# A gather, running sum and projection on one core: sums and carry by pairs of tiles in place of tile by tile, and gathers whose run-ahead grows from three pairs to eight

## The chip, the cores and the metric

The kernel runs on one core of a Trainium2 chip. The metric is the device time of one execution in microseconds (us). Several runs are taken; the median counts. The profile is that of one execution.

## The reference

For each of 16 batches, 2048 sorted row numbers pick rows of 512 floats out of 4096; the running sum over the picked rows is multiplied by a matrix of 512 x 512.

```python
B, S, N, D = (16, 4096, 2048, 512)
gathered = x[b_idx, indices, :].copy()      # (16, 2048, 512)
cs = np.cumsum(gathered, axis=1)
return np.matmul(cs, w).astype(np.float32)
```

The kernel reads 67 MB of picked rows and writes 67 MB of output.

## The kernel before

The 32,768 picked rows are cut into T = 256 tiles of P = 128 rows. Two tiles make a pair (R = 2), so there are G = 128 pairs; a batch has 16 tiles, or 8 pairs. Each engine has a list of instructions written out by hand, and a small class `Lane` puts a wait before an instruction when a semaphore must have reached a value that this engine has not yet waited for.

**POOL** (`gather`, L102 to L117) issues one indirect DMA a tile: 128 rows of x, cast to fp16 on the way, into one half of one of eight pair buffers `g16`. Tile t may be gathered when the buffer of its pair g is free, that is when `s_a` (L104) has reached 2(g+1) - 16: the sums of pair g - 8 are done. The first four tiles take their row numbers from a small early load; the others from `idxg`, which is made at the start by PE transposes (L256).

**PE** makes two kinds of matmuls. `sums(t)` (L119 to L134) multiplies the gathered tile with a mask `ut` of ones and zeros, 128 columns for each of the four 128-wide chunks of D. The result is the running sum inside the tile, transposed, in one of four PSUM buffers `pa` (NA = 4, one bank each). The columns are dealt so that even and odd output rows of the pair stand apart. The last of the four matmuls increments `s_a`. `project(g, j)` (L153 to L164) multiplies one half of the summed pair with the fp16 matrix `w16`, four matmuls of 512 columns into `pb` (NB = 2 buffers of two banks). The last one of a pair increments `s_b`.

**DVE** (`carry`, L136 to L151) adds to each tile's sums the last column of the tile before and writes fp16 into `cst`, one instruction of 128 x 512 a tile; at the first tile of a batch it only copies. It increments `s_d`. Each carry needs the one before it.

**ACT** (`drain`, L166 to L168) copies a pair's projection from `pb` to one of eight output buffers `ob` and increments `s_e`. **SP** (`store`, L170 to L174) writes it out, 512 KB a DMA.

PE's order is fixed: sums run AH = 2 pairs ahead of projections, and in the loop (L281 to L284) a tile's sums alternate with one half of a projection: `sums(2(g+2))`, `project(g,0)`, `sums(2(g+2)+1)`, `project(g,1)`. PE waits at three places: a tile's sums wait for the gather (`s_g`) and for the carry of four tiles before (L123); inside the first tile of a pair, after its first matmul, for the drain that frees the projection's buffer (`s_e`, L126); and `project(g, j)` waits for `s_d` to reach 2(g+1) + j (L154), so that the first half waits for its own pair's carries and the second half for one carry more. Where the loop ends (L285 to L295) the order is written out: first half of the last pair but two and so on, with the last two tiles' sums between them.

Of the kernel before, what the change touches and what calls it, by code (L numbers as in the profile page):

```python
# [7 lines left out]
P = 128  # L8
FP32 = mybir.dt.float32
FP16 = mybir.dt.float16  # L10
# [17 lines left out]
def kernel(  # L28
# [7 lines left out]
    nc = tc.nc  # L36

    B, S, D = x.shape
    N = indices.shape[1]
    R = 2  # L40
    Q = P // R
    DC = D // P
    NT = N // P
    T = B * NT
    G = T // R
    GB = NT // R
    KI = T // P
    FIRST = 2 * R
    NG = 16
    NA = 4  # L50
    NB = 2
    NC = 4
    NO = 8
    AH = 2
    assert D == 512 and N % (R * P) == 0 and T % P == 0

    x_flat = x.rearrange("b s d -> (b s) d")

    const = ctx.enter_context(tc.tile_pool(name="const", bufs=1))
    ps = ctx.enter_context(tc.tile_pool(name="ps", bufs=1, space=bass.MemoryType.PSUM))  # L60
# [4 lines left out]
    idxg = const.tile([P, KI, P], U32)  # L65
    w32 = const.tile([P, DC, D], FP32)
    w16 = const.tile([P, DC, D], FP16)
    ut = const.tile([P, R, Q], FP16)
    ident = const.tile([P, P], FP32)
    zeros = const.tile([P, D], FP16)  # L70
    spare = const.tile([P, 1], FP16)
    g16 = [const.tile([P, R, D], FP16, name=f"g16_{i}") for i in range(NG // R)]
    cst = [const.tile([P, DC, R, P], FP16, name=f"cst{i}") for i in range(NC)]
    ob = [const.tile([P, R, D], FP32, name=f"ob{i}") for i in range(NO)]
    pa = [ps.tile([P, DC, R, Q], FP32, name=f"pa{i}") for i in range(NA)]
    pb = [ps.tile([P, R, D], FP32, name=f"pb{i}") for i in range(NB)]

    ctx.enter_context(tc.tile_critical(no_gpsimd_drain=True))  # L78
# [1 line left out]
    def sem(name):  # L80
        return tc.alloc_semaphore(name)
# [11 lines left out]
    s_a = sem("s_a")  # L93
    s_d = sem("s_d")
# [3 lines left out]
    pool, pe, dve, act, sp = (  # L98
        Lane(e) for e in (nc.gpsimd, nc.tensor, nc.vector, nc.scalar, nc.sync)
    )  # L100

    def gather(t):  # L102
        g, r = divmod(t, R)
        pool.need(s_a, R * (g + 1) - NG)  # L104
        if t < FIRST:
            pool.need(s_first[g], 16)
            ap = idx_first[:, t, 0:1]
        else:
            pool.need(s_prep, t // P + 1)
            ap = idxg[:, t // P, t % P : t % P + 1]  # L110
        nc.gpsimd.indirect_dma_start(  # L111
            out=g16[g % (NG // R)][:, r, :],
            out_offset=None,
            in_=x_flat,
            in_offset=bass.IndirectOffsetOnAxis(ap=ap, axis=0),
            element_offset=(t // NT) * S * D,
        ).then_inc(s_g[t % NG], 16)  # L117

    def sums(t):  # L119

        g, r = divmod(t, R)
        pe.need(s_g[t % NG], 16 * (t // NG + 1))
        pe.need(s_d, t - NA + 1)  # L123
        for c in range(DC):
            if r == 0 and c == 1:
                pe.need(s_e, g - AH - NB + 1)  # L126
            mm = nc.tensor.matmul(  # L127
                out=pa[t % NA][:, c],
                lhsT=g16[g % (NG // R)][:, r, c * P : (c + 1) * P],
                rhs=ut[:],  # L130
                start=(c == 0),
                stop=(c == DC - 1),
            )
        mm.then_inc(s_a, 1)  # L134

    def carry(t):  # L136
        g, r = divmod(t, R)
        dve.need(s_a, t + 1)
        dst = cst[g % NC][:, :, :, r * Q : (r + 1) * Q]
        if t % NT == 0:  # L140
            nc.vector.tensor_copy(out=dst, in_=pa[t % NA][:]).then_inc(s_d, 1)  # L141
            return
        e = (r - 1) % R
        last = cst[(t - 1) // R % NC][:, :, R - 1, e * Q + Q - 1 : e * Q + Q]
        dve.need(s_d, t)
        nc.vector.tensor_tensor(  # L146
            out=dst,
            in0=pa[t % NA][:],
            in1=last.unsqueeze(2).broadcast_to([P, DC, R, Q]),
            op=mybir.AluOpType.add,  # L150
        ).then_inc(s_d, 1)  # L151

    def project(g, j):  # L153
        pe.need(s_d, min(R * (g + 1) + j, T))  # L154
        for c in range(DC):
            mm = nc.tensor.matmul(  # L156
                out=pb[g % NB][:, j],
                lhsT=cst[g % NC][:, c, j, :],
                rhs=w16[:, c, :],
                start=(c == 0),  # L160
                stop=(c == DC - 1),
            )
        if j == R - 1 or g == G - 1:
            mm.then_inc(s_b, 1)  # L164
# [11 lines left out]
    def drain_last(j, lane, copy):  # L176
        g = G - 1
        lane.need(s_o[g % NO], 16 * (g // NO))
        lane.need(s_b, g + j + 1)
        copy(out=ob[g % NO][:, j], in_=pb[g % NB][:, j]).then_inc(s_el[j], 1)  # L180
# [9 lines left out]
    with nc.allow_non_contiguous_dma(reason="a few indices, one per partition"):  # L190
        for k, eng in enumerate((nc.sync, nc.scalar)):
            t = k * R
            eng.dma_start(
                out=idx_first[:, t : t + R, :],
                in_=indices[0, t * P : (t + R) * P]
# [4 lines left out]
    for k in range(KI):  # L200
        nc.sync.dma_start(
            out=idx64[:, k, :], in_=idx_rows[k * P : (k + 1) * P, :]
# [8 lines left out]
    for j in range(R):  # L211
# [7 lines left out]
        out=ident[:],  # L219
        in_=ident[:],  # L220
# [3 lines left out]
        pattern=[[-1, P]],  # L224
# [3 lines left out]
        out=ut[:],  # L228
        in_=ut[:],
        compare_op=mybir.AluOpType.is_ge,  # L230
        fill=0.0,
        base=0,
        pattern=[[1, R], [R, Q]],
        channel_multiplier=-1,
    ).then_inc(s_ut, 1)
    for t in range(T):
        gather(t)
# [15 lines left out]
    for k in range(KI):  # L253
# [3 lines left out]
            out=pb[k % NB][:, 0, :P], in_=idxf[:, k, :], identity=ident[:]  # L257
# [5 lines left out]
    for c in range(DC // 2, DC):  # L263
        dve.need(s_w[c], 16)
        nc.vector.tensor_copy(out=w16[:, c, :], in_=w32[:, c, :]).then_inc(s_wc, 1)  # L265
    for t in range(T):
        carry(t)
    drain_last(0, dve, nc.vector.tensor_copy)


# [1 line left out]
    for t in range(R):  # L272
        sums(t)
    pe.need(s_prep, KI)
    pe.need(s_wc, DC)
    for j in range(R):
        project(0, j)
        sums(R + j)
    for t in range(2 * R, R * (AH + 1)):
        sums(t)  # L280
    for g in range(1, G - AH - 1):  # L281
        for j in range(R):
            sums(R * (g + AH) + j)
            project(g, j)  # L284
    pe.need(s_e, G - NB - 2)  # L285
    project(G - 3, 0)
    project(G - 3, 1)
    sums(T - 2)
# [48 lines left out]
```

## Time and profile before

| what | value |
|---|---|
| median of 3 runs | 401.83 us (401.7 to 401.89) |
| the profiled execution's own time | 401.7 us |
| its span, first to last instruction | 400.0 us |
| PE busy | 322.6 us (81%) |
| POOL busy | 241.5 us (60%) |
| DVE busy | 178.9 us (45%) |
| ACT busy | 128.4 us (32%) |
| DMA queue of the gathers | 36864 packets, 33.57 MB, 59.2% of 16 engines |
| DMA queue of the stores and loads | 19712 packets, 68.43 MB, 44.1% of 16 engines |
| mean granted PE clock | 0.917 |

The profile divides the span into 40 slices of 10 us; each digit is a share in tenths. "Idle before, releaser" in a row tells how long the engine stood still before the instruction and what ended it; "remote" and "unknown queue" mean that the profile found no instruction of this core that ended just then, and "issue" that it waited for nothing the profile shows. Matmuls overlap, so a matmul's duration is longer than its place in the stream. The shares of the two DMA queues add up to more than 100%, because packets of one engine overlap in part.

### The profile page before, as it was taken

What the parts mean: (1) busy time and instruction counts of PE and PEld (TensorE: products, weight loads), DVE (VectorE), ACT (ScalarE), POOL (GpSimd) and SP (SyncE); (2) the same over time, 40 slices, a digit from 0 to 9 for tenths busy, and PEclk for the clock granted to TensorE, in tenths of its full rate; (3) what the DMA queues carried; (4) which work ended last, traced back from release to release, by engine and by line L of the source; (5) the groups of instructions that cost most, each with busy time, mean ns of one, the idle gap of its engine ahead of it and who ended that gap; (6) DMA issues with size and microseconds to landing.
All of it is one profiled execution on the core that took longest, in us unless ns stands there. A gap on an engine that the chain in (4) does not pass through costs nothing.

```text
span 400.0 us, 5354 instructions
## 1 busy us (share of the span) xinstructions
PE 322.6 (81%) x2064; PEld 167.6 (42%) x2064; DVE 178.9 (45%) x264; ACT 128.4 (32%) x132; POOL 241.5 (60%) x264
## 2 busy tenths in 40 slices
PE   6456976797989787978789886879897898798995
PEld 2222533344544344534445443445354444354552
DVE  2214444554444454535444445554444444554552
ACT  2102423432332233233233224323332333432342
POOL 6774665666666566666666656666665765666400
PEclk9955999988989989899989899999899898988999
DMA  7986999999999999999999999999999999999985
GB/s 180 152 113 108 278 263 260 287 253 270 279 276 262 257 257 284 263 279 259 273 280 278 255 265 275 262 259 278 290 258 255 263 284 259 276 265 268 282 306 225
DMA packets 56874, 102.34 MB, mean 256 GB/s; under 512 B 6801, under 2 KB 39825, under 8 KB 56849
## 3 DMA queue, kind: packets, MB, share of 16 engines
q0 software_dynamic: 36864, 33.57, 59.2%
q1 hardware_dynamic: 19712, 68.43, 44.1%
q8 instruction: 16, 0.26, 0.3%
q14 instruction: 10, 0.07, 0.0%
q10 hardware_dynamic: 272, 0.00, 0.0%
HBM read 68.42 MB, written 67.11 MB: 339 GB/s over the span
## 4 chain that ended last, share of the span: by engine, by line
PE 74%; issue 10%; another core or an unknown queue 7%; ACT 4%; DMA 2%; DVE 1%; ACTq 0%; DVEq 0%; SPq 0%
PE pb L156 57%; PE pa L127 17%; ACT ob L168 4%; DVE cst L146 1%; DMA g<-in_x_dram,idx_first 1%; DMA idx_first<-in_indices_dram 0%; ACT ob L180 0%; ACTq L23 0%; DVEq L23 0%; SPq L332 0%; SPq L78 0%
## 5 line engine op out<-in xcount | busy, mean ns | idle before, releaser
L111 POOL DMA_INDIRECT g<-in_x_dram,idxg x252 | 236.5, 938 | 132.8 <-issue 65.3
L156 PE MATMUL pb<-w,cst 128*128 128x512 f16 x1024 | 285.3, 405 | 16.1 <-DVE cst L146 15.1
L146 DVE TENSOR_TENSOR cst<-pa,cst 128x512 f16<-128x512 f32 x240 | 166.1, 692 | 197.7 <-PE pa L127 116.4
L168 ACT COPY ob<-pb 128x1024 f32<-128x1024 f32 x127 | 125.1, 1014 | 262.2 <-PE pb L156 183.7
L127 PE MATMUL pa<-ut,g 128*128 128x128 f16 x1024 | 114.2, 229 | 54.9 <-issue 37.8
L127 PEld LDWEIGHTS pa<-ut,g 128*128 128x128 f16 x1024 | 81.0, 103 | 134.6 <-issue 70.2
L156 PEld LDWEIGHTS pb<-w,cst 128*128 128x128 f16 x1024 | 94.6, 103 | 88.0 <-DVE cst L146 17.1
L141 DVE CAST cst<-pa 128x512 f16<-128x512 f32 x16 | 10.9, 684 | 10.0 <-PE pa L127 10.0
L244 PE MATMUL pb<-zeros 128*128 128x512 f16 x14 | 5.3, 541 | 1.5 <-DVE zeros L248 1.5
L111 POOL DMA_INDIRECT g<-in_x_dram,idx_first x4 | 3.9, 986 | 2.1 <-DMA idx_first<-in_indices_dram 1.2
L244 PEld LDWEIGHTS pb<-zeros 128*128 128x128 f16 x14 | 1.7, 130 | 3.8 <-issue 1.9
L302 ACT CAST w<-w 128x512 f16<-128x512 f32 x2 | 1.2, 618 | 2.7 <-DMA w<-in_w_dram 2.7
L251 DVE CAST idxf<-idx 128x128 f32<-128x128 uint32 x2 | 0.5, 227 | 3.4 <-DMA idx<-in_indices_dram 3.4
L265 DVE CAST w<-w 128x512 f16<-128x512 f32 x2 | 0.9, 427 | 2.2 <-DMA w<-in_w_dram 1.9
L299 ACT ACT_TABLE_LOAD x1 | 1.3, 1283 | 1.5 <-SPq L78 1.5
L180 DVE COPY ob<-pb 128x512 f32<-128x512 f32 x1 | 0.7, 692 | 1.3 <-PE pb L156 1.3
L180 ACT COPY ob<-pb 128x512 f32<-128x512 f32 x1 | 0.6, 585 | 0.9 <-PE pb L156 0.9
L248 DVE MEMSET zeros<- 128x256 uint32 x1 | 0.3, 272 | 1.1 <-SPq L78 1.1
L262 DVE CAST idxg<-pb 128x128 uint32<-128x128 f32 x2 | 0.5, 286 | 0.5 <-PE pb L256 0.5
L256 PEld LDWEIGHTS pb<-ident,idxf 128*128 128x128 f32 x2 | 0.4, 207 | 0.5 <-issue 0.3
L256 PE MATMUL pb<-ident,idxf 128*128 128x128 f32 x2 | 0.5, 369 | 0.0
L215 POOL MEMSET ident<- 128x128 f32 x1 | 0.2, 204 | 0.5 <-SPq L78 0.5
(8 smaller groups left out, 1.4 us busy)
## 6 DMA issues: line engine op xcount, KB each, us to landing
out_dram<-ob SPq DMA_DIRECT2D x127, 512.0 KB
g<-in_x_dram,idxg POOLq DMA_INDIRECT x252
w<-in_w_dram SPq DMA_DIRECT2D x4, 256.0 KB
out_dram<-ob SPq DMA_DIRECT2D x2, 256.0 KB, 2.6
idx<-in_indices_dram SPq DMA_DIRECT2D x2, 128.0 KB
g<-in_x_dram,idx_first POOLq DMA_INDIRECT x4
idx_first<-in_indices_dram ACTq DMA_DIRECT2D x1, 2.0 KB, 2.1
idx_first<-in_indices_dram SPq DMA_DIRECT2D x1, 2.0 KB, 1.9
```

What stands on the lines that cost most here:

```text
L111: nc.gpsimd.indirect_dma_start(out=g16[g % (NG // R)][:, r, :], out_offset=None, in_=x_flat, in_offset=bass.IndirectOffsetOnAxis(ap=ap, ax ...
L127: mm = nc.tensor.matmul(out=pa[t % NA][:, c], lhsT=g16[g % (NG // R)][:, r, c * P : (c + 1) * P], rhs=ut[:], start=(c == 0), stop=(c == DC ...
L141: nc.vector.tensor_copy(out=dst, in_=pa[t % NA][:]).then_inc(s_d, 1)
L146: nc.vector.tensor_tensor(out=dst, in0=pa[t % NA][:], in1=last.unsqueeze(2).broadcast_to([P, DC, R, Q]), op=mybir.AluOpType.add,).then_inc ...
L156: mm = nc.tensor.matmul(out=pb[g % NB][:, j], lhsT=cst[g % NC][:, c, j, :], rhs=w16[:, c, :], start=(c == 0), stop=(c == DC - 1),)
L168: nc.scalar.copy(out=ob[g % NO][:], in_=pb[g % NB][:]).then_inc(s_e, 1)
L180: copy(out=ob[g % NO][:, j], in_=pb[g % NB][:, j]).then_inc(s_el[j], 1)
L244: nc.tensor.matmul(out=pb[NB - 1][:, R - 1], lhsT=zeros[:, :P], rhs=zeros[:], start=True, stop=True)
L256: nc.tensor.transpose(out=pb[k % NB][:, 0, :P], in_=idxf[:, k, :], identity=ident[:]).then_inc(s_pt, 1)
L265: nc.vector.tensor_copy(out=w16[:, c, :], in_=w32[:, c, :]).then_inc(s_wc, 1)
L299: nc.scalar.copy(out=spare[:], in_=zeros[:, :1])
L302: nc.scalar.copy(out=w16[:, c, :], in_=w32[:, c, :]).then_inc(s_wc, 1)
```

## The change

Sums and carry go by pairs. The mask `ut` becomes 128 x 2 x 128. The first tile of a pair multiplies with all 256 columns of it, the second with 128 columns, added to the upper half of the same `pa` buffer; the sum over 256 rows is thus made by PE. There are two `pa` buffers, each of two banks, in place of four of one. `s_a` and `s_d` now count pairs. One carry of 128 x 1024 a pair replaces two of 128 x 512. `project(g, j)` waits for the carry of pair g + j.

The gather of pair g waits for the sums of the pair min(8, 3 + g // 16) before it: three pairs for the first 16 pairs, then four for 16 pairs, and so on, and eight from pair 80.

```diff
-    NA = 4
+    EARLY = 3
+    RAMP = 16
+    NA = 2
...
-    ut = const.tile([P, R, Q], FP16)
+    ut = const.tile([P, R, P], FP16)
...
-    pa = [ps.tile([P, DC, R, Q], FP32, name=f"pa{i}") for i in range(NA)]
+    pa = [ps.tile([P, DC, R, P], FP32, name=f"pa{i}") for i in range(NA)]
...
     def gather(t):
         g, r = divmod(t, R)
-        pool.need(s_a, R * (g + 1) - NG)
+        pool.need(s_a, g + 1 - min(NG // R, EARLY + g // RAMP))
...
         pe.need(s_g[t % NG], 16 * (t // NG + 1))
-        pe.need(s_d, t - NA + 1)
+        pe.need(s_d, g - NA + 1)
+
         for c in range(DC):
             if r == 0 and c == 1:
                 pe.need(s_e, g - AH - NB + 1)
             mm = nc.tensor.matmul(
-                out=pa[t % NA][:, c],
+                out=pa[g % NA][:, c] if r == 0 else pa[g % NA][:, c, :, Q:],
                 lhsT=g16[g % (NG // R)][:, r, c * P : (c + 1) * P],
-                rhs=ut[:],
-                start=(c == 0),
-                stop=(c == DC - 1),
+                rhs=ut[:] if r == 0 else ut[:, :, :Q],
+                start=(r == 0 and c * R * P % D == 0),
+                stop=(r == R - 1 and (c + 1) * R * P % D == 0),
             )
-        mm.then_inc(s_a, 1)
-
-    def carry(t):
-        g, r = divmod(t, R)
-        dve.need(s_a, t + 1)
-        dst = cst[g % NC][:, :, :, r * Q : (r + 1) * Q]
-        if t % NT == 0:
-            nc.vector.tensor_copy(out=dst, in_=pa[t % NA][:]).then_inc(s_d, 1)
+        if r == R - 1:
+            mm.then_inc(s_a, 1)
+
+    def carry(g):
+        dve.need(s_a, g + 1)
+        dst = cst[g % NC]
+        if g % GB == 0:
+            nc.vector.tensor_copy(out=dst[:], in_=pa[g % NA][:]).then_inc(s_d, 1)
             return
-        e = (r - 1) % R
-        last = cst[(t - 1) // R % NC][:, :, R - 1, e * Q + Q - 1 : e * Q + Q]
-        dve.need(s_d, t)
+        last = cst[(g - 1) % NC][:, :, R - 1, P - 1 : P]
+        dve.need(s_d, g)
         nc.vector.tensor_tensor(
-            out=dst,
-            in0=pa[t % NA][:],
-            in1=last.unsqueeze(2).broadcast_to([P, DC, R, Q]),
+            out=dst[:],
+            in0=pa[g % NA][:],
+            in1=last.unsqueeze(2).broadcast_to([P, DC, R, P]),
             op=mybir.AluOpType.add,
         ).then_inc(s_d, 1)
...
     def project(g, j):
-        pe.need(s_d, min(R * (g + 1) + j, T))
+        pe.need(s_d, min(g + 1 + j, G) if g else 1)
...
-        pattern=[[1, R], [R, Q]],
+        pattern=[[1, R], [R, P]],
...
-    for t in range(T):
-        carry(t)
+    for g in range(G):
+        carry(g)
```

More of the change, by code (lines that the diff above doesn't have):

```diff
@@ L54 @@
     AH = 2
-    assert D == 512 and N % (R * P) == 0 and T % P == 0
+    assert R == 2 and D == 512 and N % (R * P) == 0 and T % P == 0
     x_flat = x.rearrange("b s d -> (b s) d")
```

## The prediction

> **What bounds the kernel now.** I read the account of the 40 slices first, then stretches of 4 us at the start and one long stretch after it, then the timeline, and last the groups for durations.
>
> The page's second section says which engine is full, and when:
>
> ```profile
> PE   6456976797989787978789886879897898798995
> POOL 6774665666666566666666656666665765666400
> PEclk9955999988989989899989899999899898988999
> DMA  7986999999999999999999999999999999999985
> ```
>
> Only the DMA row stands at 9 from slice 4 to slice 37 (counted from 0); PE goes up and down between 6 and 9. The holes of the DMA row are at both ends. The stretches (columns: busy time of PE, PEld, DVE, ACT, POOL, with instruction counts; then granted clock, DMA share, GB/s) put numbers on it:
>
> ```profile
> 4.00:8.00 4.00, 2.89 (x11) 1.23 (x9) 0.71 (x3) 1.24 (x2) 3.08 (x4) 1.00 1.00 284
> 8.00:12.00 4.00, 1.97 (x16) 1.09 (x16) 2.15 (x4) 0.00 (x0) 2.96 (x4) 1.00 0.98 147
> 12.00:16.00 4.00, 1.99 (x22) 1.29 (x20) 0.69 (x1) 1.01 (x1) 2.91 (x4) 1.00 0.86 103
> 16.00:20.00 4.00, 1.19 (x4) 0.52 (x5) 0.69 (x1) 0.00 (x0) 3.08 (x4) 0.90 1.01 227
> 20.00:24.00 4.00, 3.08 (x13) 1.32 (x11) 0.69 (x1) 0.00 (x0) 3.08 (x4) 0.50 0.88 119
> 24.00:28.00 4.00, 0.04 (x1) 0.05 (x2) 0.69 (x1) 0.00 (x0) 3.09 (x4) 0.50 0.86 106
> 28.00:32.00 4.00, 2.27 (x8) 0.90 (x8) 0.00 (x0) 0.00 (x0) 1.91 (x3) 0.50 0.83 102
> 32.00:36.00 4.00, 1.74 (x5) 0.65 (x6) 2.18 (x4) 1.01 (x1) 1.18 (x2) 0.50 0.15 24
> 36.00:40.00 4.00, 4.00 (x18) 1.98 (x17) 1.97 (x3) 1.01 (x1) 3.09 (x4) 0.54 1.00 202
> 40.00:380.00 340.00, 285.85 (x1872) 150.00 (x1871) 160.57 (x234) 115.01 (x117) 215.25 (x230) 0.93 1.09 269
> 380.00:400.00 20.00, 15.02 (x99) 7.70 (x97) 8.02 (x12) 7.67 (x8) 0.00 (x0) 0.95 0.69 265
> ```
>
> For 340 us the 16 DMA engines stand at 1.09 (packets overlap a little). I take 1.09 as full, since no stretch of 20 us shows more. The whole DMA work is then 340 x 1.09 + 1.5 (0 to 4 us) + 30.3 (4 to 40, nine stretches) + 13.8 (380 to 400) = 416 share-us, which is 382 us at full rate. The span of 400.0 us has 18 us of lost DMA time: 2.6 before 4 us, 36 - 30.3/1.09 = **8.2 from 4 to 40 us**, and 20 - 13.8/1.09 = **7.3 after 380 us**. So the middle can give almost nothing to a change that moves the same bytes, and the ends can.
>
> What goes wrong from 14 to 36 us is in the timeline (start, duration, engine, line):
>
> ```profile
> 29.64 0.63 PE L127 MATMUL pa<-ut,g 128*128 128x128 f16 x4
> ...
> 33.51 3.88 DVE L146 TENSOR_TENSOR cst<-pa,cst 128x512 f16<-128x512 f32 x5 [5.61 <-remote]
> ...
> 34.34 1.01 ACT L168 COPY ob<-pb 128x1024 f32<-128x1024 f32 x1 [19.10 <-remote]
> 34.52 0.94 POOL L111 DMA_INDIRECT g<-in_x_dram,idxg  x1 [4.00 <-remote]
> ```
>
> PE had finished the sums of tiles 6, 7, 8 and 9 at 15.1, 20.8, 24.0 and 30.3 us (the n-th sum against the n-th carry), yet DVE starts tile 6 only at 33.51, and then five carries run without a gap. ACT starts a drain at 34.34 whose projection ended at 23.6. PE's increments reach DVE, ACT and POOL late and in a burst. POOL issues gathers without a stop from 3.2 to 30.5 us, and the burst comes after it has stood still. The same, smaller, repeats every 8.8 us in the middle: POOL issues six gathers, 1.24 us apart, then stands about 1.6 us, and the late increments arrive then:
>
> ```profile
> 204.65 1.49 DVE L146 TENSOR_TENSOR cst<-pa,cst 128x512 f16<-128x512 f32 x2 [2.16 <-remote]
> 204.76 1.93 ACT L168 COPY ob<-pb 128x1024 f32<-128x1024 f32 x2 [3.33 <-PE pb L156]
> 204.88 0.94 POOL L111 DMA_INDIRECT g<-in_x_dram,idxg  x1 [1.64 <-remote]
> ```
>
> After POOL's last gather (376.38 us) the delay is gone: every carry follows its sum by 0.04 us, and PE needs 2.17 us for a pair. I read this as: while POOL issues without a pause, PE's increments lag (in the updates of s_a and s_b they come 1.44 us apart in the middle, 2.8 to 6.3 apart at the start). Why, the trace does not say.
>
> **The change, part by part.** Durations are from this profiled execution: 401.7 us with 400.0 of span, so 1.7 lie outside the span; the median of the three runs is 401.83.
>
> *PE.* The 8 projection matmuls of a pair stay (0.86 us for four, as L156 stands in the chain). The sums had eight of 128 columns, 0.22 us for four. The first tile of a pair now streams 256 columns, the second 128: 0.44 + 0.22 in place of 0.44, so **+0.22 us a pair**, 2.17 to 2.39. Over 128 pairs that is 28 us of PE work. In the middle a pair takes 8.82 / 3 = 2.94 us, of which some 0.75 is PE idle or slowed, so it lies beside the DMA. In the last six pairs, where PE sets the pace, it shows: 6 x 0.22 = 1.3 us. If the cover is gone, all 25 us of the middle show (rival 2).
>
> *DVE.* Two instructions of 692 ns a pair become one of 128x1024. Between L262 (128 columns, 286 ns) and L141 (512 columns, 684 ns) lies 1.04 ns a column, so 692 + 512 x 1.04 = 1.22 us; twice 692 is the upper bound. DVE is 45% busy. But its result comes at once: a pair's carry is 0.5 us later than the second half's was.
>
> *Waits.* pa is two buffers of a pair. Second projections wait for the next pair's carry. From the end of a pair's sums to that wait PE still has 0.86 + 0.44 + 0.86 + 0.22 = 2.38 us; less 1.22 for the carry leaves 1.15 us for a late increment, against 3.24 - 0.69 = 2.55 before. Behind PE's wait stand all later sums and projections, and behind them ACT's drains and POOL's next gathers. In return PE sends two increments a pair in place of three. At 1.44 us each that is 2.88 us a pair in place of 4.32, against 2.94 of time: just enough, so I take no new stall. The price is between 0 and rival 2's.
>
> *The end.* Before, the second projection of the last pair but one waited for tile 254's carry. Now it waits for the carry of the last pair, whose sums stand directly ahead of it: 1.22 + 0.1 = 1.3 us of PE standing still. With the 1.3 above the end is **2.6 us longer**.
>
> *Gathers.* Same 256 instructions, 1.24 us each. A pair may be issued when the pair three before it is summed (four from pair 16, then five, eight from pair 80). At the start POOL must stop after pair 3, at about 13 us, until pair 1 is summed, and from then on once a pair. By the rows above, increments flow when it stops. The loop over three pairs is: second gather issued 1.25 after the first, landed 6.1 after its issue (gathers' semaphore updates from 40 us on; 3.1 to 3.6 while gathers run alone), sum 0.25, increment 0.1 to 1.4: 7.7 to 9.0 us, or 2.6 to 3.0 a pair against 2.93 at full DMA. So up to 1.1 us are lost in 16 pairs, and the first ten microseconds after 4 keep their loss of 10 - 9.64/1.09 = 1.2. I take 2.7 us lost in place of 8.2: **5.5 us gained**. Bounds: 0 if the throttle itself starves the DMA or the stall is not POOL's doing, 7.0 if only the 1.2 stays.
>
> A rule against this part stands in the Trainium skill, "DMA: Bandwidth & Descriptors", section "Rules for kernel authors": issue a DMA early and wait for it late, so that its fixed cost is hidden. Here gathers are summed 18 to 20 us after their issue and land within 8, so the row leaves room to issue later; by the rule alone the throttle gains nothing and the time would be 404.4. The skill's "Perfetto Trace Analysis", section on the Tensor Engine instruction, says that a matmul's increment is pushed when PSUM has acknowledged the writes and then propagates; no figure there covers the 4 to 18 us that this trace shows.
>
> *Sum.* 400.0 - 5.5 + 2.6 = 397.1 of span, + 1.7 outside it, and 0.1 from this run to the median: **399.0 us**; with the bounds of the start, 397 to 404.5.
>
> **Rivals.**
> 1. *The increments flow in the middle too.* With two a pair the queue never builds, PE stays close to the gathers, the DMA runs at 1.12 as in its best stretches of 4 us (44 to 48, 76 to 80), and 340 us become 331; the end has one pair less to catch up, some 2 us. 399 - 9 - 2 = 388. For: the tail without gathers shows PE needs only 2.17. Against: no 20 us of this run hold more than 1.09.
> 2. *PE becomes the bound (slower).* Its place is the wait of the second projection for the carry; it decides once increments lag by more than 1.15 us, and they lag by 2 to 4 us now in each cycle. If the 2.3 us of lost PE time in each three pairs stay while its work grows by 0.66, a pair takes 3.16 us: 113 x 0.22 = 25 us, so 399 + 25 - 1 = 423; if half of the added 0.66 is taken up by shorter stalls, 411. For: the lags of this trace. Against: a third of the increments is gone, and with ready data PE is 0.5 us a pair faster than the DMA.
> 3. *The throttle does not do it.* If the stall at the start comes from something else than POOL's run-ahead, or a lead of three is as slow, only the longer end is left: 404.4. For: increments at 9 to 14 us were prompt while POOL already issued. Against: after 376 us, and after each stop.
>
> **How the numbers follow.** Three runs lie within 0.05%, so about 0.2%, 0.8 us, is what can be told from no change. Forecast 0.42 (0.35 of it below 401.0, 0.05 within, 0.02 above); rival 1 0.17; rival 2 0.26; rival 3 0.12; in between, as before, 0.03. Faster 0.52, same 0.08, slower 0.40. The range runs from rival 1's 388 to 415: it leaves out the full price of rival 2 (about 0.12) and what lies under 388 (0.07).
>
> **What would show it.** Right: no DMA slice under 8 from slice 1 to slice 37, pair 16 summed by 60 us (before: 66.6), no gap of 19 us between ACT's first drains, carries following sums within 1.2 us, and a PE pause of 1.3 us at the very end. Wrong: DMA share in the middle under 1.05 with PE waiting for L146's successor (rival 2), a DMA hole between 14 and 60 us (rival 3), or POOL standing still with the DMA not full.

## The result, and the profile after

The changed kernel takes 407.59 us (median; 406.86 to 407.75) where the kernel before takes 401.86 beside it: ratio 1.0131, 95% interval 1.0105 to 1.0157. It is 5.7 us slower; 399.0 was forecast, 2.8 us faster. The profiled execution has a span of 406.0 us.

Section 2 of the page of the changed kernel (40 slices of 10.15 us):

```profile
PE   6778968888698778878699886888878878888893
POOL 6466666666665675566656665666566666666100
PEclk9699999999989998999979998999999999999999
DMA  7599999999999999999999999999999999999954
```

The hole of the DMA row at the start has moved from slices 2 and 3 (counted from 0) to slice 1, and the row then stays at 9 up to slice 37. The PE row, though, dips to 6 in slices 5, 10, 19 and 24. What lies in such dips is shown below.

The stretches of the changed kernel (busy time of PE, PEld, DVE, ACT, POOL, with counts; then clock, DMA share, GB/s):

```profile
4.00:8.00 4.00, 3.54 (x11) 1.39 (x9) 1.00 (x4) 1.24 (x2) 3.08 (x4) 1.00 0.99 294
8.00:12.00 4.00, 1.33 (x8) 0.66 (x8) 1.55 (x3) 0.00 (x0) 2.22 (x4) 0.79 0.99 139
12.00:16.00 4.00, 3.13 (x10) 1.46 (x11) 0.72 (x1) 0.00 (x0) 1.61 (x2) 0.50 0.71 91
16.00:20.00 4.00, 3.25 (x24) 1.86 (x22) 2.35 (x2) 1.01 (x1) 1.88 (x2) 0.86 0.24 67
20.00:24.00 4.00, 3.25 (x24) 1.65 (x23) 1.34 (x3) 1.01 (x1) 2.82 (x4) 1.00 1.02 177
24.00:28.00 4.00, 3.13 (x20) 1.51 (x18) 1.21 (x1) 1.01 (x1) 2.81 (x3) 1.00 1.05 225
28.00:32.00 4.00, 2.67 (x18) 1.32 (x16) 1.93 (x2) 1.01 (x1) 2.05 (x3) 1.00 0.92 202
32.00:36.00 4.00, 3.92 (x25) 2.09 (x24) 1.74 (x2) 2.02 (x2) 3.08 (x4) 1.00 1.09 255
36.00:40.00 4.00, 2.97 (x21) 1.54 (x22) 1.22 (x1) 1.01 (x1) 2.07 (x3) 1.00 1.09 280
40.00:380.00 340.00, 282.10 (x1789) 157.33 (x1787) 136.91 (x112) 112.95 (x112) 217.97 (x233) 0.97 1.08 262
380.00:400.00 20.00, 18.68 (x120) 10.44 (x119) 8.57 (x7) 8.17 (x9) 0.00 (x0) 1.00 0.66 247
```

The DMA share of the 340 us is 1.08 where it was 1.09, and yet they carry 262 GB/s in place of 269. Part of that difference is only work done earlier: by 40 us the changed kernel has moved 7.2 MB, the kernel before 5.6.

This table has the times between the ends of certain pairs' sums, in us. The first two columns are from the executions above; the other four are profiles of the second set of runs, told of below. Each column adds up to its span.

| stretch | before | after | before (again) | after (again) | pairs, lead 8, end freed | tiles, ramp |
|---|---|---|---|---|---|---|
| start to pair 16 | 67.7 | 62.4 | 68.4 | 62.8 | 70.6 | 62.5 |
| pair 16 to pair 80 | 188.1 | 197.6 | 191.4 | 199.5 | 188.9 | 201.6 |
| pair 80 to pair 121 | 121.7 | 120.8 | 122.3 | 120.2 | 122.7 | 120.4 |
| pair 121 to the end | 22.5 | 25.2 | 23.1 | 27.0 | 23.8 | 26.3 |
| span | 400.0 | 406.0 | 405.2 | 409.5 | 406.0 | 410.8 |

By this table the start gained 5.3 us, the end lost 2.7, and pairs 16 to 80 lost 9.5, for which nothing had been put down. From pair 80 on, where the lead is eight in both kernels, the pace is the same (2.95 us a pair, 2.97 before) though PE has 0.22 us a pair more to do.

But the two kernels are not equally far when pair 16's sums end, because one gathers further ahead than the other. Both have 256 gathers to issue, so these are counted here for the same six columns:

| gathers | before | after | before (again) | after (again) | pairs, lead 8, end freed | tiles, ramp |
|---|---|---|---|---|---|---|
| issued when pair 16's sums end | 46 | 39 | 46 | 40 | 47 | 38 |
| issued from there until pair 80's sums end | 128 | 136 | 128 | 135 | 127 | 136 |
| us for each of these | 1.47 | 1.45 | 1.50 | 1.48 | 1.49 | 1.48 |
| 25th issued at, us | 37.00 | 40.60 | 36.89 | 39.80 | 37.19 | 42.42 |
| last issued at, us | 376.38 | 378.45 | 379.89 | 380.38 | 379.86 | 383.75 |
| from there to the end, us | 23.6 | 27.6 | 25.3 | 29.2 | 26.1 | 27.1 |

So the 5.3 us are no lasting gain: seven gathers fewer have been issued by then. They are made up while the lead grows: eight more gathers at 1.45 us are 11.6 us, more than the 9.5 that pairs 16 to 80 lost. The pace of a gather there is no slower than before. Counted by gathers, the changed kernel is 3.6 us behind at the 25th, before the lead has risen at all, still 2.1 behind at the last, and loses another 4.0 from there to the end.

A usual cycle of the changed kernel, from its timeline:

```profile
283.69 0.94 POOL L113 DMA_INDIRECT g<-in_x_dram,idxg  x1 [0.31 <-issue]
...
285.47 0.39 PE L130 MATMUL pa<-ut,g 128*128 128x128 f16 x4
286.05 1.22 DVE L144 CAST cst<-pa 128x1024 f16<-128x1024 f32 x1 [3.71 <-PE pa L130]
...
286.29 0.94 POOL L113 DMA_INDIRECT g<-in_x_dram,idxg  x1 [1.65 <-PE pa L130]
...
287.33 1.04 PE L158 MATMUL pb<-w,cst 128*128 128x512 f16 x4 [1.48 <-DVE cst L144]
```

After six gathers POOL stands 1.65 us, the late increments arrive, and PE goes on after 1.48 us of waiting. The cycle is 8.8 us for three pairs, as before. Now the same kernel where the lead rises from five pairs to six (the gathers of pair 48 were issued at 145.3 us):

```profile
148.92 1.22 DVE L148 TENSOR_TENSOR cst<-pa,cst 128x1024 f16<-128x1024 f32 x1 [3.68 <-PE pa L130]
149.08 0.94 POOL L113 DMA_INDIRECT g<-in_x_dram,idxg  x1 [0.30 <-issue]
...
150.32 0.94 POOL L113 DMA_INDIRECT g<-in_x_dram,idxg  x1 [0.31 <-issue]
151.07 0.27 PE L130 MATMUL pa<-ut,g 128*128 128x256 f16 x1
151.56 0.94 POOL L113 DMA_INDIRECT g<-in_x_dram,idxg  x1 [0.30 <-issue]
152.51 1.01 ACT L170 COPY ob<-pb 128x1024 f32<-128x1024 f32 x1 [6.56 <-PE pb L158]
153.57 0.77 PE L130 MATMUL pa<-ut,g 128*128 128x256 f16 x3 [2.23 <-issue]
...
154.64 1.23 DVE L148 TENSOR_TENSOR cst<-pa,cst 128x1024 f16<-128x1024 f32 x1 [4.49 <-remote]
...
154.87 0.94 POOL L113 DMA_INDIRECT g<-in_x_dram,idxg  x1 [2.37 <-remote]
```

POOL has room for one pair more and issues ten gathers, from 140.38 to 151.56, before it stands. Pair 45's sums ended at 148.75, their carry starts at 154.64: 5.9 us late, where a usual cycle has at most 2.6. ACT gets no projection for 6.6 us, and PE stands inside a tile until ACT has drained. It is the stall of the start in small. Ten gathers then take 14.5 us (140.38 to 154.87), 1.45 each, where six take 8.8 in a usual cycle. The stall comes at each rise: pairs that take over 6 us are 33, 46, 62 and 77 in the changed kernel, and none elsewhere after pair 1; pair 14, at the first rise, takes 5.0.

### The profile page after: what moved, and what is told of

Same layout as the page of the kernel before. It is cut to its first block, busy times and chain, and to the rows that moved or that the text cites. A ratio compares the mean times of both kernels' runs of the same rounds, so it can differ in the third digit from the quotient of the medians.

```text
span 406.0 us, 5095 instructions
## 1 busy us (share of the span) xinstructions
PE 331.5 (82%) x2064; PEld 182.3 (45%) x2064; DVE 159.5 (39%) x136; ACT 131.8 (32%) x132; POOL 241.7 (60%) x264
## 4 chain that ended last, share of the span: by engine, by line
PE 71%; issue 13%; DMA 6%; POOL 4%; DVE 3%; another core or an unknown queue 1%; SPq 1%; ACT 0%; ACTq 0%
PE pb L158 51%; PE pa L130 20%; DMA g<-in_x_dram,idxg 5%; POOL g L113 4%; DVE cst L148 2%; DMA w<-in_w_dram 1%; DVE cst L144 1%; DVE w L267 0%; SPq L203 0%; SPq L207 0%; ACT ob L182 0%; SPq L195 0%; SPq L334 0%; ACTq L23 0%
## 5 line engine op out<-in xcount | busy, mean ns | idle before, releaser
L113 POOL DMA_INDIRECT g<-in_x_dram,idxg x252 | 236.4, 938 | 134.9 <-issue 66.6
L158 PE MATMUL pb<-w,cst 128*128 128x512 f16 x1024 | 269.3, 387 | 48.6 <-issue 36.6
L148 DVE TENSOR_TENSOR cst<-pa,cst 128x1024 f16<-128x1024 f32 x112 | 137.2, 1225 | 203.1 <-PE pa L130 125.6
L170 ACT COPY ob<-pb 128x1024 f32<-128x1024 f32 x127 | 128.5, 1012 | 264.9 <-PE pb L158 171.1
L130 PE MATMUL pa<-ut,g 128*128 128x256 f16 (+1 forms) x1024 | 130.3, 250 | 19.4 <-issue 11.3
L130 PEld LDWEIGHTS pa<-ut,g 128*128 128x128 f16 x1024 | 88.8, 99 | 90.8 <-issue 26.5
L144 DVE CAST cst<-pa 128x1024 f16<-128x1024 f32 x16 | 19.6, 1223 | 27.7 <-PE pa L130 18.7
```

What stands on the lines that cost most here:

```text
L113: nc.gpsimd.indirect_dma_start(out=g16[g % (NG // R)][:, r, :], out_offset=None, in_=x_flat, in_offset=bass.IndirectOffsetOnAxis(ap=ap, ax ...
L130: mm = nc.tensor.matmul(out=pa[g % NA][:, c] if r == 0 else pa[g % NA][:, c, :, Q:], lhsT=g16[g % (NG // R)][:, r, c * P : (c + 1) * P], r ...
L144: nc.vector.tensor_copy(out=dst[:], in_=pa[g % NA][:]).then_inc(s_d, 1)
L148: nc.vector.tensor_tensor(out=dst[:], in0=pa[g % NA][:], in1=last.unsqueeze(2).broadcast_to([P, DC, R, P]), op=mybir.AluOpType.add,).then_ ...
L158: mm = nc.tensor.matmul(out=pb[g % NB][:, j], lhsT=cst[g % NC][:, c, j, :], rhs=w16[:, c, :], start=(c == 0), stop=(c == DC - 1),)
L170: nc.scalar.copy(out=ob[g % NO][:], in_=pb[g % NB][:]).then_inc(s_e, 1)
```

## The experiments

Each ratio is against the kernel before on the same chip. The chips were of two kinds. In the result above and in the second set of runs the kernel before takes 402 to 406 us, with increments that come late. In the four other sets, each on another chip, it takes 356.5 to 356.9 us, and there carries follow their sums by 0.04 us, a few at the start aside. I call the two kinds **delayed** and **prompt**. They were not to be chosen.

**The halves of the change, first set, a prompt chip.** By pairs without the ramp, the ramp on single tiles, and a lead of three pairs throughout:

```diff
 pairs_lead8 (against the changed kernel)
-        pool.need(s_a, g + 1 - min(NG // R, EARLY + g // RAMP))
+        pool.need(s_a, g + 1 - NG // R)
 tiles_ramp (against the kernel before)
-        pool.need(s_a, R * (g + 1) - NG)
+        pool.need(s_a, R * (g + 1 - min(NG // R, 3 + g // 16)))
 pairs_lead3
+        pool.need(s_a, g + 1 - EARLY)
 tiles_lead3
+        pool.need(s_a, R * (g + 1 - 3))
```

> Sums and carry by pairs, gathers eight pairs ahead from the first one on: the change without its ramp. Theory A (the loss in the middle comes from the steps of the ramp: pairs 33, 46, 62 and 77 of the changed kernel take 6.4 to 8.5 us each, and there the lead has just grown): the middle runs at 8.82 us in three pairs as before, the start gains nothing, the end is 2.7 us longer: about 404.5 us. Theory B (pairing itself costs the middle, by more PE work and a shallower pa): the middle loses 8.6 us and the start gains nothing, about 413 us.

Measured: 358.33 us against 356.56, ratio 1.0055 (1.0034 to 1.0076).

> Sums and carry by single tiles as before, but gathers run 3 pairs ahead at first and one pair more every 16 pairs, up to 8: the ramp alone. Theory A: the start gains 5 us, the steps cost 8 to 9 us, about 405 us. Theory B: only the gain at the start is left, about 396.5 us.

Measured: 360.18, ratio 1.0105 (1.0081 to 1.0129).

> The changed kernel with a lead of three pairs to the end, no steps. Theory A: no pair takes over 5 us after pair 20, the start gains 5 us, the end costs 2.7 or less: 398 to 401 us if a lead of three feeds the DMA (pairs 3 to 13 of the changed kernel went at 2.99 us), so up to 405. Theory B: 408 us or more.

Measured: 388.42, ratio 1.0861 (1.0818 to 1.0904).

> Sums and carry by single tiles, with a lead of three pairs to the end. Theory A: the start gains 5 us, nothing is lost at steps nor at the end: 395 to 398 us. Theory B: the same, since neither pairs nor more PE work are in it; if a lead of three is too short for the DMA, over 402 us under both.

Measured: 385.76, ratio 1.0852 (1.0786 to 1.0919).

None of the expected times fits, since they were made for the delayed kind: a prompt chip has neither the stall at the start nor that at a rise, so these four can't tell A from B. What they show is the price of a short lead where nothing else is in the way. The ramp alone costs 1.05%, and not at its rises: from pair 16 to 80 tiles_ramp takes 168.1 us and pairs_lead8 169.1, each with 135 gathers, while pair 16 is summed at 57.3 us in the one and 53.6 in the other. A lead of three throughout costs 8.5%, with tiles as with pairs. The waits of pairs_lead3 tell why (who waited for whom: us in total, times, longest):

```profile
PEld pa L130 <- DMA g<-in_x_dram,idxg: 98.4, 123, 2.8
POOL g L113 <- PE pa L130: 79.2, 100, 3.2
```

PE waits for the gather and POOL for PE, in a ring. A pair takes 2.86 us (pair 20 at 69.55 us, pair 120 at 355.91), where pairs_lead8 needs 2.64 (63.70 to 327.55): in the upper half of the 2.6 to 3.0 that the prediction's loop gave.

**Both kernels and both halves, second set, a delayed chip.** pairs_lead8_end is pairs_lead8 and also lets the second half of the last pair but one go ahead of the last carry:

```diff
-        pe.need(s_d, min(g + 1 + j, G) if g else 1)
+        pe.need(s_d, (g + 1 + j if g < G - 2 else g + 1) if g else 1)
```

> The kernel before, unchanged, for a profile on the chip on which the other kernels of this call run. The first four experiments ran on a chip on which this kernel takes 356.6 us and in whose traces every carry follows its sum by 0.04 us. Two kinds of behaviour are thus to be told apart: increments of PE delayed while POOL issues (402 us), or prompt (356 us). On a chip of the prompt kind I expect no standing still of PE from 15 to 34 us and pair 16 summed by 54 us; on the other kind a repeat of the first profile.

Measured: 406.91 us; the median of the kernel before on this chip is 405.73 over 19 runs. PE again stands at the start: pair 4 takes 11.25 us. The expectations for this kind were made from 401.9 us, so they are to be read as differences.

> The changed kernel, unchanged. Theory A (steps of the ramp): where increments are delayed, 407 us again, with the long pairs at the steps. Where they are prompt, the costs of the two halves add up: 356.6 + 1.8 (pairs alone) + 3.6 (ramp alone) = 362 us. Theory B (pairing costs the middle): 407 us where delayed; on a prompt chip 360 to 362 as well.

Measured: 411.57, ratio 1.0127 (1.0079 to 1.0175), 5.8 us over: the result again. The long pairs are 14 (6.1 us), 32, 45, 60 and 76 (7.6 to 8.6).

> The change without its ramp, and with the second half of the last pair but one projected without waiting for the last carry: tells what the wait at the end costs. On a prompt chip 0.9 us under the version without the ramp (the 0.86 us of that half lie beside the carry), so about 357.4 where before takes 356.6. Where increments are delayed: theory A 403.5 us, theory B 412 us.

Measured: 407.43, ratio 1.0030 (1.0012 to 1.0048). No pair after pair 5 takes over 5 us, and pairs 16 to 80 take 188.9 us where the kernel before takes 191.4 on this chip. **Pairing costs nothing in the middle.** Theory A had put this version 1.6 us over the kernel before, B 10; it is 1.7 by the medians, 1.2 by the ratio. Theory B falls.

> The ramp alone on single tiles, again, beside the kernel before on this chip. Where increments are delayed: theory A about 405 us (start 5 us better, steps 8 to 9 us worse), theory B 396.5. On a prompt chip 360 us as before.

Measured: 408.65, ratio 1.0062 (1.0042 to 1.0082). Theory A had put it 3.1 us over, B 5.4 under; it is 2.9 over by the medians, 2.5 by the ratio. The ramp alone makes the kernel slower, with single tiles as with pairs: pairs 32, 46, 62 and 75 take 6.9 to 9.8 us. The rise at pair 48 in the timeline of tiles_ramp_again, whose profiled execution lies 3.9 us above its median:

```profile
151.95 0.94 POOL L111 DMA_INDIRECT g<-in_x_dram,idxg  x1 [0.30 <-issue]
152.34 0.22 PE L127 MATMUL pa<-ut,g 128*128 128x128 f16 x1
154.01 0.69 DVE L146 TENSOR_TENSOR cst<-pa,cst 128x512 f16<-128x512 f32 x1 [4.25 <-remote]
154.25 0.94 POOL L111 DMA_INDIRECT g<-in_x_dram,idxg  x1 [1.36 <-remote]
...
155.88 0.50 PE L127 MATMUL pa<-ut,g 128*128 128x128 f16 x3 [3.32 <-issue]
```

It is the same stall, after the gathers of pair 48, in a kernel without pairs. In the first table, the three columns with a ramp take 198 to 202 us from pair 16 to 80, the three without 188 to 191. That agrees with theory A, but it does not show that the stall makes the price: by the second table the three with a ramp issue 7 to 9 gathers more in that stretch, at the pace of the others, and their 25th gather, before any rise, is already 2.6 to 5.5 us later than in the kernels without a ramp of the same set. The two halves also add up: 1.0062 for the ramp, 1.0030 for pairs, and some 0.9 us (0.0022) for the wait at the end that pairs_lead8_end leaves out (an estimate: one half projection, 0.86 us) make 1.0114; 1.0127 was measured.

**A lead that never rises.** If the rises are to blame, a constant lead of four should keep the gain at the start. By tiles it ran three times, by pairs once, each time on a prompt chip:

```diff
 tiles_lead4
-        pool.need(s_a, R * (g + 1) - NG)
+        pool.need(s_a, R * (g + 1 - 4))
 pairs_lead4 (against the changed kernel)
-        pool.need(s_a, g + 1 - min(NG // R, EARLY + g // RAMP))
+        pool.need(s_a, g + 1 - 4)
```

> Single tiles as before, gathers four pairs ahead from the first to the last, so there is neither the long run of POOL at the start nor a step. Theory A (every rise of the lead is paid for by a time in which POOL issues without a stop and PE's increments wait): where increments are delayed the start's gain stays, 5 to 8 us under before, and no pair after pair 10 takes over 6 us. Rival (a short lead starves the DMA, or the ramp is neutral): no gain, or a loss. On a chip with prompt increments: the stretches with a lead of four in the ramp run at 2.66 us a pair like those with eight, so within 2 us of before.

> The changed kernel with a lead of four pairs from the first to the last. Theory A: the version by tiles with the same lead plus the cost of pairing, 2 to 3 us more than that one; where increments are delayed 3 to 5 us under before and 8 to 10 under the changed kernel. Rival B (pairing costs the middle): 8 us more than the version by tiles.

Measured: tiles 358.70 against 356.49, ratio 1.0049 (1.0027 to 1.0071). Pairs 360.38, ratio 1.0111 (1.0085 to 1.0137). One pair more of lead takes back nearly all of the 8.5%; pairing costs 0.6% here too.

> Single tiles, a lead of four pairs from first to last, again. Where increments are delayed: theory A (each rise of the lead is paid for) 5 to 8 us under before and no pair after pair 10 over 6 us; rival (short lead starves the DMA, the rise is not the cause): no gain. On a prompt chip 0.5% over before, as seen.

> Single tiles, a lead of four pairs from first to last, a third time. Where increments are delayed: theory A 5 to 8 us under before, no pair after pair 10 over 6 us; rival: no gain. On a prompt chip 0.5% over before.

Measured: 358.15, ratio 1.0048 (1.0023 to 1.0074), and 358.29, ratio 1.0049 (1.0027 to 1.0072). From pair 16 to 80 the three runs by tiles take 166.9 to 167.4 us with 128 gathers, where tiles_ramp takes 168.1 with 135: on a prompt chip seven gathers more cost about 1 us. What a constant four does on a delayed chip stays open, and with it whether a version there beats the kernel before.

**Is it POOL's issuing or the load of the DMA engines that delays the increments?** Two kernels, each with an eighth of the bytes in one direction; x_small is the same memory in rows of 64 numbers, and gathers_small also clears the rest of each tile once at the start:

```diff
 stores_small
-        nc.sync.dma_start(out=dst, in_=ob[g % NO][:]).then_inc(s_o[g % NO], 16)
+        nc.sync.dma_start(out=dst[:, :, : P // 2], in_=ob[g % NO][:, :, : P // 2]).then_inc(s_o[g % NO], 16)
 gathers_small
-            out=g16[g % (NG // R)][:, r, :],
+            out=g16[g % (NG // R)][:, r, : P // 2],
-            in_=x_flat,
+            in_=x_small,
```

> The kernel before, but each store writes the first 64 of 512 columns of a pair's rows alone: the same number of DMAs with an eighth of the bytes. Theory C (PE's increments wait because POOL issues gathers, whatever the DMA engines carry): on a chip with delayed increments the delays and the three-pair period near 8.8 us stay, 400 us or little less. Theory D (the DMA engines' load sets the pace and the delays): delays go, a pair takes POOL's 2.49 us, about 340 us. On a prompt chip: near 340 us, POOL's pace.

> The kernel before, but each gathered row is 64 numbers in place of 512 (other numbers than the reference's; the rest of the tile is zero): the same 256 gathers with the same 128 descriptors each and an eighth of the bytes. Theory C: where increments are delayed, delays and period stay, about 400 us. Theory D: delays go, about 340 us. On a prompt chip near 340 us.

> Stores of 64 of 512 columns, an eighth of the bytes. Prompt chips gave 335.6 us, POOL's pace. Where increments are delayed: theory C (POOL's issuing delays them, whatever the DMA carries) near 400 us; theory D (the load of the DMA engines) near 340.

> Gathers of 64 numbers a row in place of 512 (other numbers than the reference's), as many descriptors. Prompt chips gave 336.1 us. Where increments are delayed: theory C near 400 us; theory D near 340.

> Stores of 64 of 512 columns. Prompt chips 335.5 us. Where increments are delayed: theory C (POOL's issuing delays them, whatever the DMA carries) near 400 us; theory D (load of the DMA engines) near 340.

> Gathers of 64 numbers a row in place of 512 (other numbers than the reference's), as many descriptors. Prompt chips 336 us. Where increments are delayed: theory C near 400 us; theory D near 340.

Measured: 335.57, 335.33 and 336.12 us with small stores, 336.09, 336.03 and 336.75 with small gathers, all on prompt chips. So these runs do **not settle** the question: no delayed chip ran them. The first profile of the kernel before speaks against the load. Its last gather is issued at 376.38 us, and then:

```profile
376.00:380.00 4.00, 3.92 (x30) 2.27 (x31) 3.24 (x6) 1.95 (x3) 1.01 (x2) 1.00 1.10 316
380.00:384.00 4.00, 4.00 (x32) 2.31 (x31) 2.48 (x4) 2.02 (x2) 0.00 (x0) 1.00 1.06 374
```

The DMA engines move 374 GB/s, where the 340 us before 380 have 269, and every carry from 379.7 us on follows its sum by 0.04 us; from 24 to 32 us they move 102 to 106, and the carries that start from 27.2 to 35.1 us are 11 to 18 us late. So traffic alone does not delay them. On the prompt chips POOL issues at the same pace and they are not late, so its issuing is not enough either.

The runs with small traffic show what bounds a prompt chip and what the DMA share is worth. The same stretch of 280 us in four kernels, first the kernel before on its delayed chip, then on prompt chips pairs_lead8, stores_small and gathers_small:

```profile
40.00:320.00 280.00, 233.68 (x1537) 122.73 (x1536) 130.72 (x190) 94.03 (x96) 179.15 (x192) 0.94 1.09 268
```

```profile
40.00:320.00 280.00, 267.73 (x1705) 140.11 (x1706) 130.78 (x107) 107.34 (x107) 207.86 (x222) 1.00 1.13 300
```

```profile
40.00:320.00 280.00, 260.69 (x1807) 128.85 (x1806) 155.82 (x226) 114.40 (x113) 211.35 (x226) 1.00 0.97 133
```

```profile
40.00:320.00 280.00, 254.17 (x1802) 132.69 (x1801) 155.61 (x226) 113.93 (x113) 211.34 (x226) 1.00 0.76 225
```

A share of 0.97 goes with 133 GB/s in one kernel, 1.13 with 300 in another. So the recorded time of the packets does not follow the bytes. With either traffic cut, POOL's own pace is left: 226 gathers in 280 us, 1.24 us each. With both whole a prompt chip takes 6% longer (356.5 us), so there the transfers hold POOL up.

## Why the prediction was wrong

**The step that failed is *Gathers*.** It took the 5.5 us of the start as gained and put down nothing for what follows: "a pair may be issued when the pair three before it is summed (four from pair 16, then five, eight from pair 80)" stands there, but the four pairs by which the lead still grows after pair 16 got no term in the sum. A shorter lead puts gathers off and does not save them. The runs showed in its place: pair 16 was summed 5.3 and 5.6 us earlier, with 39 and 40 gathers issued in place of 46; from pair 16 to 80 the changed kernel took 9.5 and 8.1 us more, with eight and seven gathers more, at 1.45 and 1.48 us each. In gathers nothing was gained. The 25th came 3.6 and 2.9 us later than before, the last 2.1 and 0.5, and with the longer end the span grew by 6.1 and 4.4 us. The kernel before pays for its lead of eight once, at the start; the ramp pays for it in instalments.

The ramp alone makes the kernel slower on both kinds of chip; that is shown. The price of the four rises after pair 16, 8 to 10 us, is no more than the added gathers take at their usual pace. On a prompt chip seven such gathers cost about 1 us. That on a delayed chip they cost their full time fits the prediction's own reading, by which PE's increments lag while POOL issues without a pause; but that the stall is the reason is argued and not shown, and why an increment waits for POOL is not known.

**The gain at the start was right in its number and not in its reason, so the match is luck.** 5.5 us were to come from lost DMA time, 2.7 in place of 8.2 from 4 to 40 us. By the same reckoning the nine rows of the changed kernel from 4 to 40 us, with 32.4 us of DMA share, have 36 - 32.4/1.09 = 6.3 lost. (The 2.7 was a choice: the two losses that the text gives, 1.1 and 1.2, make 2.3.) What the loop over three pairs left out is its first round:

```profile
17.78 0.94 POOL L113 DMA_INDIRECT g<-in_x_dram,idxg  x1 [3.87 <-PE pa L130]
```

Pair 1's first gather was issued at 5.90 us and its sums ended at 17.50, 11.6 us later in place of 7.7 to 9.0; in between PE projected pair 0, at a clock of 0.50 from 12 to 16 us. So pair 4's gather came at 17.78 us, where the kernel before issued it at 13.42. After that the loop ran at 2.85 us a pair up to pair 12 (40.60 us), inside the 2.6 to 3.0 forecast; the kernel before, with its stop, needed 2.95. Pair 16 was to be summed by 60 us; it was at 62.4, and at 67.7 before (the prediction's 66.6 is the end of its first tile). Of the five signs of being right two came: no long gap between ACT's first drains, and PE's pause at the end.

**The end was right in its pause, and in the rest by luck**: 2.6 us forecast, 2.7 measured after pair 121, 3.9 in the second set. But tiles_ramp_again, whose end is as before, is 3.2 us longer there too, so a match to 0.1 us in that stretch says little; from the last gather on the changed kernel takes 4.0 and 3.9 more. The pause itself, in the changed kernel:

```profile
396.47 0.39 PE L130 MATMUL pa<-ut,g 128*128 128x128 f16 x4
...
396.90 1.23 DVE L148 TENSOR_TENSOR cst<-pa,cst 128x1024 f16<-128x1024 f32 x1 [2.89 <-PE pa L130]
...
398.18 2.76 PE L158 MATMUL pb<-w,cst 128*128 128x512 f16 x12 [1.32 <-DVE cst L148]
```

The carry takes 1.23 us (1.22 forecast), and PE stands 1.32 us for it (1.3 forecast).

**PE and the waits were right, and rival 2 wrong**: 0.22 us a pair came (2.39 between sums that wait for nothing), and a usual cycle kept its 8.8 us; PE's lost time in it fell from 2.3 to 1.6 us (8.8 less three pairs' work). The carries are up to 2.6 us late, past the 1.15 us of slack, and PE does wait for them, but the cycle's length is not set by that wait. Rival 1 did not come. Rival 3 (404.4: nothing gained at the start, only the longer end left; chance 0.12) came nearest: its sign, a DMA hole between 14 and 60 us, is there (0.24 from 16 to 20), and the lead of three did feed the gathers no better than before. The prediction's own sum, 400.0 - 5.5 + 2.6 + 1.8, is 398.9.

**"I take 1.09 as full" was wrong as an argument.** The same work runs at 300 GB/s and a share of 1.13 on a prompt chip, and a share of 0.97 goes with 133 GB/s. A share near 1 told that the engines held packets, not that they could carry no more. It led to "the middle can give almost nothing", and what the middle would have to pay was not asked.

## What to carry to other kernels

A limit on run-ahead that changes is a series of events: put a term into the sum for each change of it, not only for the first. Compare two versions where they have the same work behind them: if one runs further ahead, count what it has issued before calling the other one's lead a gain. Before shortening a lead, work out the ring it closes (issue, landing, use, release, over the pairs in it) and keep a pair above what the pace needs; here three was 8.5% too slow and four within 0.5% on a prompt chip. A high busy share of DMA engines is no proof that they bound: look at the GB/s of other stretches and of other runs.

## What the runs showed of the hardware

One and the same kernel took 356.5 to 356.9 us on four chips, 405.7 on another, and 401.9 where the result was taken: 13 to 14% more. In the traces of the fast four, carries start 0.04 us after the modelled end of their sums; in the others up to some 4 us late in a usual cycle, 5.3 to 8.5 at the rises after pair 16 and up to 18 at the start, while POOL issues gathers 1.24 us apart. From 2 to 7 us after POOL's last gather on they are at 0.04 again. Whether the chip itself or its state at that time sets the two kinds apart is not known.
